# Linear attention by pairs of token tiles, with the output gates applied where the output projection's operand is made

## The chip, the cores and the metric

The kernel runs on one core of a Trainium2 chip. The metric is the time of one execution in device microseconds; the time before is the median of three runs. The engines are named as in the profile: PE (matmul; PEld its weight loads), DVE (elementwise, vector), ACT (activation functions and copies), POOL, and SP, which here issues most DMAs.

## The reference

One encoder layer for 1024 prompt tokens and 64 sample tokens (1088 in all, width 1024). A modulated RMS norm, one input projection, two mixers side by side, one output projection, and a squared-ReLU MLP of 4096. What matters here is the second mixer, gated linear attention with 4 heads, keys of 64 and values of 128, and what follows it:

```
b = cumsum(log_a); scores = q k exp(b_t - b_s), causal
o = scores v + (q exp(b)) state
state = state exp(b_end) + (k exp(b_end - b))^T v
o = rms_norm(o) * silu(r)
x = x + gate1 * (concat[attention, o] @ w_out)
```

Everything is float32; large products are made of three products of rounded halves.

## The kernel before

Activations lie with features on the partitions. Tokens are worked in tiles of 128 (`TILES`, eight of the prompt and one of 64 for the sample). Large matmuls go through `mm3` (L91 to L95): each operand is split into a rounded high part (ACT copy, L101) and a rest (DVE difference, L102), and three matmuls add up.

The order of the work is made by `interleave` (L46). Each stream of work is a generator that yields an estimate of PE time, a wait, and a condition; the first stream in the list that may go on goes on. The stage in question (L842) has the streams weights, `gla` (linear attention), `main` (projection of values and gate inputs, groups B0 and B1), `gate_cols` (projection of r, groups C0 and C1, stored to the DRAM tensor `r_d`), `gates`, and `latents` (group D1, which may run on into the next stage). The framework then orders the instructions of each queue from this priority and their dependences; the engines and SP work their queues in order. `load_group` (L195) brings a weight group through three raw buffers and splits it into one of two operand buffers.

`gla` works one tile at a time. `main` gives it the cumulated log gates `bcum`. For each of seven levels (halves of 64, 32, ... 1 tokens) `prep` forms the difference of b to a reference (L686), its exponentials for keys (L691) and, by head halves, for queries (L694), and multiplies them with keys (L696) and queries (L703). The query operand `QL` holds zeros in the other head's half of the partitions, so that one matmul serves two heads. Two matmuls (L755) give scores, of which a masked copy (L763; for the first level an ACT copy, L760) puts the blocks that belong to this level into `ST`. After the levels come the output (L798, L802), its norm (L807 to L810), and in `tail` a transposition and a store to the DRAM tensor `mix_d` (L816 to L820). The recurrent state is updated at the third level (L775 to L784).

`gates` (L828) waits for all of that in the planner, and then, tile by tile, loads r and the mix from DRAM, makes silu (L837) and product (L838), and stores the mix again (L839). The two loads use the buffers of the values (`gv`).

The next stage makes the keys of the past (`past_keys`: transposition L1074, split L1080 and L1081, products in `keys_values`) and the query latents (`query_main`). Then follows attention. Near its end `out_early` (L1190) loads the first quarter of the mix (272 tokens) in three pieces into the raw buffers, splits them, and begins four column blocks of the output projection while attention ends. The other three quarters are loaded (L1326, L1327), split (L1344, L1345) and multiplied in `main` of the output projection (L1319).

## Time and profile before

| what | us |
|---|---|
| median of three runs (1381.74 to 1384.07) | 1383.76 |
| the profiled execution's own time | 1381.47 |
| its span | 1379.7 |
| PE busy in the span | 1333.5 |
| DVE busy | 903.7 |
| ACT busy | 700.6 |
| PE busy from 95 to 285 (190 us, linear attention) | 186.35 |
| PE busy from 285 to 330 (45 us, its end and the next stage's begin) | 27.53 |
| PE busy from 440 to 600 (160 us, attention) | 157.00 |
| PE busy from 600 to 700 (100 us, output projection) | 100.00 |

A busy PE is a matmul in flight; the stretch that stands out is the one from 285 to 330. In the profile's rows a group shows its line, engine, operation, output and inputs with their shapes, the count, the busy time and the mean of one, and then the idle time of the engine before them with what ended it.

### The profile page before, as it was taken

To read this page: it belongs to the slowest core of one execution; us is meant where nothing else is said; L and a number is where in the kernel's file an instruction comes from. 1 tells how busy PE (TensorE), PEld (TensorE's weight loads), DVE (VectorE), ACT (ScalarE), POOL (GpSimd) and SP (SyncE) were. 2 spreads that over 40 slices of the span, in tenths; PEclk is the share of its full clock that TensorE was granted. 3 is DMA by queue.
4 is the path that set the end of the run, shared out by engine and by line. 5 is a ranking of instruction groups with operands and counts; after the bars stand their busy time and mean duration, and the time that the engine had idled before them with its cause. 6 is when DMAs were issued, how large, how long until landed. Compare 5 with 4: busy or idle time off the path is not lost.

```text
span 1379.7 us, 26169 instructions
## 1 busy us (share of the span) xinstructions
PE 1333.5 (97%) x10020; PEld 1256.7 (91%) x10020; DVE 903.7 (65%) x2041; ACT 700.6 (51%) x1768; POOL 61.9 (4%) x115
## 2 busy tenths in 40 slices
PE   7999999959999999999999999999999999999998
PEld 5898899948866779899999999999999999999998
DVE  5787876746475756756799756656645866864554
ACT  5466766963255656744474444444434343434332
POOL 0010000111011110000000000000000000000000
PEclk9999999989999999999999999999999999999999
DMA  9420315552154431364406444444249855543440
GB/s 344 127 74 1 89 55 151 151 153 81 58 176 125 160 113 41 85 187 128 139 23 204 161 133 160 136 142 154 97 160 322 277 197 168 174 124 99 123 130 33
DMA packets 166167, 188.14 MB, mean 136 GB/s; under 512 B 16878, under 2 KB 117530, under 8 KB 166042
## 3 DMA queue, kind: packets, MB, share of 16 engines
q1 hardware_dynamic: 158586, 180.90, 41.6%
q10 hardware_dynamic: 7456, 5.57, 1.3%
q8 instruction: 79, 1.29, 0.4%
q14 instruction: 46, 0.38, 0.1%
HBM read 132.97 MB, written 53.46 MB: 135 GB/s over the span
## 4 chain that ended last, share of the span: by engine, by line
PE 83%; DVE 6%; ACT 4%; DMA 3%; issue 2%; POOL 1%; SPq 0%; ACTq 0%; DVEq 0%; POOLq 0%
PE mm L93 15%; PE mm L95 14%; PE mm L94 14%; PE g L93 6%; PE g L95 6%; PE g L94 5%; PE tp L93 3%; PE tp L95 3%; PE tp L94 3%; PE mm L1000 3%; PE g L1027 2%; PE mm L166 2%; PE g L755 1%; PE tp L1037 1%; DVE al L102 1%
## 5 line engine op out<-in xcount | busy, mean ns | idle before, releaser
L101 ACT CAST opers<-quad 128x512 fp32r<-128x512 f32 x112 | 69.5, 621 | 184.6 <-PE mm L95 145.0
L102 DVE TENSOR_TENSOR opers<-quad,opers 128x512 fp32r<-128x512 f32 x112 | 77.2, 690 | 113.7 <-ACT opers L101 113.7
L93 PE MATMUL mm<-opers 128*128 128x272 f32 x448 | 128.7, 287 | 0.3 <-DVE e L1816 0.3
L95 PE MATMUL mm<-opers 128*128 128x272 f32 x448 | 128.9, 288 | 0.0
L94 PE MATMUL mm<-opers 128*128 128x272 f32 x448 | 128.3, 286 | 0.0
L93 PE MATMUL mm<-ah,wh 128*128 128x272 f32 x424 | 122.4, 290 | 2.7 <-ACT wh L101 1.3
L94 PE MATMUL mm<-al,wh 128*128 128x272 f32 x424 | 121.6, 288 | 0.3 <-DVE al L102 0.3
L95 PE MATMUL mm<-ah,wl 128*128 128x272 f32 x424 | 121.5, 288 | 0.0
L93 PE MATMUL mm<-hh,wh 128*128 128x384 f32 (+2 forms) x264 | 91.8, 350 | 0.3 <-ACT hh L101 0.3
L94 PE MATMUL mm<-hl,wh 128*128 128x384 f32 (+2 forms) x264 | 88.0, 333 | 0.0
L95 PE MATMUL mm<-hh,wl 128*128 128x384 f32 (+2 forms) x264 | 87.4, 331 | 0.0
L93 PEld LDWEIGHTS mm<-opers 128*128 128x128 f32 x448 | 84.6, 189 | 0.5 <-issue 0.5
L95 PEld LDWEIGHTS mm<-opers 128*128 128x128 f32 x448 | 84.3, 188 | 0.0
L94 PEld LDWEIGHTS mm<-opers 128*128 128x128 f32 x448 | 84.1, 188 | 0.0
L93 PEld LDWEIGHTS mm<-ah,wh 128*128 128x128 f32 x424 | 79.8, 188 | 4.0 <-ACT wh L101 1.9
L94 PEld LDWEIGHTS mm<-al,wh 128*128 128x128 f32 x424 | 79.7, 188 | 0.5 <-DVE al L102 0.5
L95 PEld LDWEIGHTS mm<-ah,wl 128*128 128x128 f32 x424 | 79.5, 188 | 0.2 <-DVE wl L102 0.2
L102 DVE TENSOR_TENSOR opers<-ru,opers 128x544 fp32r<-128x544 f32 x108 | 77.6, 719 | 2.2 <-ACT opers L101 2.0
L101 ACT CAST opers<-ru 128x544 fp32r<-128x544 f32 x108 | 69.5, 644 | 13.1 <-PE mm L95 11.7
L101 ACT CAST wh<-ru 128x512 fp32r<-128x512 f32 x67 | 41.2, 618 | 65.3 <-PE g L94 24.5
L102 DVE TENSOR_TENSOR wl<-ru,wh 128x512 fp32r<-128x512 f32 x67 | 45.9, 689 | 35.6 <-ACT wh L101 35.4
L93 PE MATMUL mm<-wh,hh 128*128 128x264 f32 (+3 forms) x216 | 66.8, 311 | 0.0
(410 smaller groups left out, 4316.7 us busy)
## 6 DMA issues: line engine op xcount, KB each, us to landing
ru<-u_d SPq DMA_DIRECT2D x108, 272.0 KB, 2.9
raw<-in_w_ada SPq DMA_DIRECT2D x40, 512.0 KB, 3.9
ru<-in_w_up SPq DMA_DIRECT2D x32, 512.0 KB, 4.2
quad<-in_w_down SPq DMA_DIRECT2D x16, 1024.0 KB, 7.6
u_d<-st SPq DMA_DIRECT2D x60, 272.0 KB, 2.1
u_d<-sc SPq DMA_DIRECT2D x45, 272.0 KB, 2.1
raw<-in_w_in SPq DMA_DIRECT2D x22, 256.0 KB, 4.6
x<-in_xo_T SPq DMA_DIRECT2D x8, 544.0 KB, 5.4
```

The lines of the kernel that those rows point to most:

```text
L93: PE.matmul(out, lhsT=ah, rhs=bh, start=first, stop=False, skip_group_check=more)
L94: PE.matmul(out, lhsT=ah, rhs=bl, start=False, stop=False, skip_group_check=more)
L95: PE.matmul(out, lhsT=al, rhs=bh, start=False, stop=last, skip_group_check=more)
L101: ACT.copy(hi, src)
L102: eng.tensor_tensor(out=lo, in0=src, in1=f32(hi), op=ALU.subtract)
L166: mm = PE.matmul(acc[32 * j:32 * j + 32, 0:256], lhsT=scT[:, k, :], rhs=was[k][:, 256 * j:256 * (j + 1)], start=(k == 0), stop=(k == KT - ...
L755: PE.matmul(sc[:n, p, :, :n // 2], lhsT=kl[:, n * p:n * p + n], rhs=ql[:, :, p, :n // 2], start=True, stop=True)
L1000: PE.matmul(sp[:n, :w], lhsT=x[:, hd, :n], rhs=y[:, hd, :w], start=(j == 0), stop=(j == 4))
L1027: PE.matmul(op[:n, 0:P], lhsT=pt[:kw, k, :n], rhs=kvs[kt // 4].v[:kw, kt % 4, hd], start=(kt == 0), stop=(kt == nkt - 1))
L1037: PE.transpose(tp[:kw, k, :n], pr[k0 // 4][:n, P * k:P * k + kw], ident[:n, :n])
```

## The change

The linear attention takes two tiles in one turn (`UNITS`; the sample's tile alone). `prep` makes one difference over both tiles and two exponentials in place; `factors` multiplies the key part in place and writes the query part, head half by head half, into zero-padded `QL` buffers of full length; four matmuls fill a whole bank with scores of both tiles, and one masked copy takes them. The state is updated between the tiles of a pair. `main` projects B1 (gates and half of the values) before B0, and marks values and gates apart. q and k are laid out by pairs, so that an eviction of 384 columns is written in pieces. `load_group` issues its raw loads before it waits for operand buffers. The stream `gates` is gone: `out_early` and the output projection's `main` load r beside the mix and apply silu and product before they split the operand; in `out_early` the operand comes in six pieces instead of three. The core of the diff:

```diff
+UNITS = [(0, 1), (2, 3), (4, 5), (6, 7), (8,)]
...
-    def load_group(key, src, nk, n, step=2, after=None, pool=None):
-
-        if after is not None:
-            yield 300, 0, after
-        wh = (pool or wp).tile([P, nk, n], F32R, name="wh")
-        wl = (pool or wp).tile([P, nk, n], F32R, name="wl")
+    def load_group(key, src, nk, n, step=2, after=None, pool=None, early=None):
+
         units = [(k, min(step, nk - k)) for k in range(0, nk, step)]
         raws = {}
 
...
             raws[u] = rawp.tile([P, kn, n], F32, name="raw")
             SP.dma_start(raws[u], src[k * P:(k + kn) * P].rearrange("(k p) n -> p k n", p=P))
 
+        if early is not None:
+            yield 300, 0, early
         for u in range(min(3, len(units))):
             load(u)
         yield 0, 4000, None
+        if after is not None:
+            yield 0, 0, after
+        wh = (pool or wp).tile([P, nk, n], F32R, name="wh")
+        wl = (pool or wp).tile([P, nk, n], F32R, name="wl")
...
-    GROUPS = [("A0", 704, 960), ("A1", 960, 1216), ("B0", 1216, 1480), ("B1", 1480, 1744), ("C0", 1744, 2000),
+    GROUPS = [("A0", 704, 960), ("A1", 960, 1216), ("B1", 1480, 1744), ("B0", 1216, 1480), ("C0", 1744, 2000),
               ("C1", 2000, 2256), ("D1", 384, 704)]
 
     def loader():
         for j, (key, a, b) in enumerate(GROUPS):
             if j >= 2:
-                yield from load_group(key, w_in_cols(a, b), 8, b - a, after=has("end " + GROUPS[j - 2][0]))
+                yield from load_group(key, w_in_cols(a, b), 8, b - a, after=has("end " + GROUPS[j - 2][0]),
+                                      early=has("shift") if j == 2 else None)
         yield from load_group("UK", I["w_ukv"], 2, 1024, step=1, after=has("end C1"))
-        yield from load_group("UQ", I["w_uq"], 3, 768, step=1, after=has("end D1"))
+        yield from load_group("UQ", I["w_uq"], 3, 768, step=1, early=has("end D1"))
...
-                        ACT.activation(qk_place((i + 2) % 4, c0, c0 + cn), by_tile(ps, c0), AF.Copy,
-                                       scale=0.125 if g == 0 else 1.0)
+                        for a, b in pieces(c0, c0 + cn):
+                            ACT.activation(qk_place((i + 2) % 4, a, b), ps[:, a - c0:b - c0], AF.Copy,
+                                           scale=0.125 if g == 0 else 1.0)
...
-        KL = [big.tile([P, 2 * P], F32, name=f"KL{j}") for j in range(3)]
-        QL = [big.tile([P, 2, 2, 64], F32, name=f"QL{j}") for j in range(3)]
         SBk = [big.tile([P, 2, 256], F32, name=f"SB{i}") for i in range(3)]
-        for t in KL + QL + SBk:
+        QL = [big.tile([P, 2, 2 * P], F32, name=f"QL{j}") for j in range(2)]
+        for t in QL + SBk:
...
         def main():
-            yield 0, 0, has("B0")
+            turn = 0
+            yield 0, 0, has("B1")
             for c in range(3):
                 c0, cn = CHUNKS[c]
                 tl = [(i, off, n) for i, (off, n) in enumerate(TILES) if c0 <= off < c0 + cn]
-                for i, off, n in tl:
-                    ps = yield from rows("B0", off, n, 264)
-                    gvs[i] = gw.tile([P, 512], F32, name="gv", bufs=9)
-                    ACT.copy(gvs[i][:n, 0:264], ps)
-                yield 1500, 0, has("B1")
-                glr = glrT[c % 2]
-                for part in (tl[:1], tl[1:]) if c == 0 else (tl,):
+                for part in (tl[:2], tl[2:]) if c < 2 else (tl,):
+                    glr = glrT[turn % 2]
+                    turn += 1
+                    t0, tn = part[0][1], sum(n for _, _, n in part)
                     for i, off, n in part:
                         ps = yield from rows("B1", off, n, 264)
-                        DVE.tensor_copy(gvs[i][:n, 264:512], ps[:, 0:248])
-                        gl = sm.tile([P, 16], F32, name="gl")
+                        gvs[i] = gw.tile([P, 512], F32, name="gv", bufs=7)
+                        gl = spare[:, 16 * (i % 4):16 * (i % 4) + 16]
                         DVE.tensor_copy(gl[:n], ps[:, 248:264])
+                        ACT.copy(gvs[i][:n, 264:512], ps[:, 0:248])
                         tp = tp_bank()
                         PE.transpose(tp[0:16, 0:n], gl[:n], ident[:n, :n])
-                        DVE.tensor_copy(glr[0:16, off - c0:off - c0 + n], tp[0:16, 0:n])
-                    t0, tn = part[0][1], sum(n for _, _, n in part)
+                        DVE.tensor_copy(glr[0:16, off - t0:off - t0 + n], tp[0:16, 0:n])
                     for p in range(2):
                         z = g_bank()
-                        PE.matmul(z[:, :tn], lhsT=wg[:, p * P:(p + 1) * P], rhs=glr[:, t0 - c0:t0 - c0 + tn],
+                        PE.matmul(z[:, :tn], lhsT=wg[:, p * P:(p + 1) * P], rhs=glr[:, 0:tn],
                                   start=True, stop=True)
                         a = gw.tile([P, 384], F32, name="sq")
                         ACT.activation(a[:, :tn], z[:, :tn], AF.Abs)
...
                             DVE.tensor_tensor_scan(bcum[:, p, off:off + n], ones[:, :n], a[:, off - t0:off - t0 + n],
                                                    0.0, op0=ALU.mult, op1=ALU.add)
                     done.update(f"gates {i}" for i, _, _ in part)
+                for i, off, n in tl:
+                    yield 0, 0, has("B0")
+                    ps = yield from rows("B0", off, n, 264)
+                    ACT.copy(gvs[i][:n, 0:264], ps)
+                    done.add(f"v {i}")
...
                 def prep(hf):
 
 
+                    bv = b.rearrange("p c (x y) -> p c x y", y=2 * hf)
+                    ref = bv[:, :, :, hf - 1:hf].broadcast_to([P, 2, w // (2 * hf), 2 * hf])
+                    d = gw.tile([P, 4 * P], F32, name="dd", bufs=3)[:, 0:2 * w]
+                    DVE.tensor_tensor(out=d.rearrange("p (c x y) -> p c x y", c=2, y=2 * hf), in0=bv, in1=ref, op=ALU.subtract)
+                    dv = d.rearrange("p (x r h) -> p x r h", r=2, h=hf)
+                    for r in range(2):
+                        ACT.activation(dv[:, :, r], dv[:, :, r], AF.Exp, scale=(2 * r - 1) / 16.0)
+                    return d, hf
+
+                def factors(d, hf):
+
                     nonlocal rot
-                    bv = b.rearrange("p c (x y) -> p c x y", y=2 * hf)
-                    ref = bv[:, :, :, hf - 1:hf].broadcast_to([P, 2, n // (2 * hf), 2 * hf])
-                    dd = gw.tile([P, 2 * P], F32, name="dd", bufs=3)[:, 0:2 * n]
-                    DVE.tensor_tensor(out=dd.rearrange("p (c x y) -> p c x y", c=2, y=2 * hf), in0=bv, in1=ref, op=ALU.subtract)
-                    ds, dt = roles(dd, hf)
-                    kl, ql = KL[rot % 3][:, 0:2 * n], QL[rot % 3]
+                    ql = QL[rot % 2]
                     rot += 1
-                    ks, _ = roles(kl, hf)
-                    ACT.activation(ks, ds, AF.Exp, scale=-1.0 / 16)
+                    dv = d.rearrange("p (x r h) -> p x r h", r=2, h=hf)
+                    kv, qv = (kq[:, 2 * w * r:2 * w * r + 2 * w].rearrange("p (x r h) -> p x r h", r=2, h=hf)[:, :, r]
+                              for r in range(2))
+                    DVE.tensor_tensor(out=dv[:, :, 0], in0=dv[:, :, 0], in1=kv, op=ALU.mult)
                     for j in range(2):
-                        ps = slice(64 * j, 64 * j + 64)
-                        ACT.activation(ql[ps, j, :, :n // 2].rearrange("p c (b h) -> p c b h", h=hf),
-                                       dt[ps].rearrange("p (c b) h -> p c b h", c=2), AF.Exp, scale=1.0 / 16)
-                    DVE.tensor_tensor(out=ks, in0=roles(kq[:, 0:2 * n], hf)[0], in1=ks, op=ALU.mult)
-                    qt = roles(kq[:, 2 * n:4 * n], hf)[1]
-                    for c in ((0, 2),) if n == P else ((0, 1), (1, 2)):
-                        c0, c1 = c
-                        qv = ql[:, :, c0:c1, :n // 2].rearrange("p j c (b h) -> p j (c b) h", h=hf)
-                        nb = n // (2 * hf)
-                        q1 = qt[:, c0 * nb:c1 * nb].rearrange("p (o x) h -> p o x h", o=1).broadcast_to([P, 2, (c1 - c0) * nb, hf])
-                        DVE.tensor_tensor(out=qv, in0=qv, in1=q1, op=ALU.mult)
-                    return kl, ql
-
-                pr = gw.tile([P, 2, P], F32, name="pr", bufs=1)
-                DVE.tensor_tensor(out=pr[:, :, :n], in0=q, in1=k, op=ALU.mult)
+                        rs = slice(64 * j, 64 * j + 64)
+                        DVE.tensor_tensor(out=ql[rs, j, 0:w].rearrange("p (x h) -> p x h", h=hf), in0=dv[rs, :, 1],
+                                          in1=qv[rs], op=ALU.mult)
+                    return d, ql
...
+                kts = []
+                yield 300, 1000, None
+                for lv, hf in enumerate(halves):
+                    (d, ql), nb = ready.pop(0), n // (2 * hf)
+                    if lv + 2 < len(halves):
+                        ready.append(prep(halves[lv + 2]))
+                    if lv + 1 < len(halves):
+                        ready[0] = factors(*ready[0])
+                    if lv + 2 == len(halves):
+                        if u + 1 < len(UNITS) and can(u + 1)():
+                            begun = begin(u + 1)
+                    elif lv + 1 == len(halves) and begun is not None:
+                        begun[6][0] = begun[3](*begun[6][0])
+                        begun[6].append(begun[2](begun[5][1]))
+                    sc = g_bank()[:, 0:2 * w].rearrange("p (a c j t) -> p a c j t", a=nt, c=2, j=2)
+                    qv = ql[:, :, 0:w].rearrange("p j (c a t) -> p j c a t", c=2, a=nt)
+                    for a in range(nt):
+                        for p in range(2):
+                            PE.matmul(sc[:n, a, p], lhsT=d[:, w * p + n * a:w * p + n * a + n], rhs=qv[:, :, p, a],
+                                      start=True, stop=True)
+                    src = sc[:n].rearrange("p a c j (b h) -> p (a c j) b h", h=hf)
+                    to = ST[:n, 0:nt, :, :n].rearrange("p a g t -> p (a g) t").rearrange("p g (b r h) -> p r g b h", r=2, h=hf)[:, 1]
+                    if nb == 1:
+                        ACT.copy(to[:hf], src[:hf])
+                    else:
+                        mlv = 5 - (hf.bit_length() - 1)
+                        DVE.copy_predicated(to, masks[:n, mlv, :n // 2].rearrange("p (o b h) -> p o b h", o=1, h=hf)
+                                            .broadcast_to([n, 4 * nt, nb, hf]), src)
+                    yield 900, 2200, None
+                    if lv < nt:
+                        tp = tp_bank()
+                        for p in range(2):
+                            PE.transpose(tp[:n, P * p:P * p + P], kk[:, p, n * lv:n * lv + n], ident)
+                        kts.append(gw.tile([P, 256], F32, name="kt_", bufs=2))
+                        ACT.copy(kts[lv][:n], tp[:n, 0:256])
+                    if lv == 2:
+                        i = tl[0]
+                        yield 0, 0, has(f"v {i}")
+                        olds = (SBk[2], SBk[1]) if i == 8 else (SBk[i % 2], SBk[(i + 1) % 2])
+                        state(i, n, 0, E1, kts[0], *olds)
+                    if lv >= 3 and tails:
+                        tail()
...
-        def gates():
-
-            yield 0, 2000, has("end C1", "gla out")
-            for i, (off, n) in enumerate(TILES):
-                r, mx = (gw.tile([P, 512], F32, name="gv", bufs=9) for _ in range(2))
-                SP.dma_start(heads(r)[:, :, :n], r_d[:, :, off:off + n])
-                SP.dma_start(heads(mx)[:, :, :n], mix_d[:, 4:8, off:off + n])
-                yield 0, 1000, None
-                r, mx = (heads(t)[:, :, :n] for t in (r, mx))
-                ACT.activation(r, r, AF.Silu)
-                (DVE if i % 2 else DVE).tensor_tensor(out=r, in0=r, in1=mx, op=ALU.mult)
-                SP.dma_start(mix_d[:, 4:8, off:off + n], r)
-
         lats = Stream(latents())
-        interleave([weights, gla(), main(), gate_cols(), gates(), lats], rest=(weights, lats))
+        interleave([weights, gla(), main(), gate_cols(), lats], rest=(weights, lats))
...
+    def gate(t, r):
+        ACT.activation(r, r, AF.Silu)
+        DVE.tensor_tensor(out=t, in0=t, in1=r, op=ALU.mult)
+
     def out_early():
         yield 1000, 0, has("wo 4")
         mixh.append(wctx.enter_context(tc.tile_pool(reuse_waits="tile", name="mixh", bufs=1, side="right")))
         mh, ml = mix_pair()
         mixh.append((mh, ml))
-        ks = ((0, 3), (3, 3), (6, 2))
-        raws = []
-        for k, kn in ks:
+        def fetch(src, k, kn):
             t = rawp.tile([P, kn, HW], F32, name="raw")
-            SP.dma_start(t, mix_d[:, k:k + kn, 0:HW])
-            raws.append(t)
+            SP.dma_start(t, src[:, k:k + kn, 0:HW])
+            return t
+
+        def halves(k, kn, t):
+            split(mh[:, k:k + kn], ml[:, k:k + kn], t, DVE)
+
+        t0, t1, r1 = fetch(mix_d, 0, 3), fetch(mix_d, 4, 2), fetch(r_d, 0, 2)
         yield 0, 3000, None
-        for (k, kn), t in zip(ks, raws):
-            split(mh[:, k:k + kn], ml[:, k:k + kn], t, DVE)
+        halves(0, 3, t0)
+        gate(t1, r1)
+        halves(4, 2, t1)
+        t2, r2, t3 = fetch(mix_d, 6, 2), fetch(r_d, 2, 2), fetch(mix_d, 3, 1)
+        yield 0, 3000, None
+        gate(t2, r2)
+        halves(6, 2, t2)
+        halves(3, 1, t3)
...
+                mx.append(xw.tile([P, 4, HW], F32, name="mr", bufs=1))
                 for _, t0, n, o in parts:
+                    SP.dma_start(mx[2][:, :, o:o + n], r_d[:, :, t0:t0 + n])
...
+                    gate(mx[1], mx[2])
```

225 lines of the change are left out of this document (110 added, 115 removed).

## The prediction

> **What bounds the kernel now.** I read the page first, then the busy time of each engine by stretches, then PE's waits where PE is not full, then the order of time there.
>
> ```profile
> span 1379.7 us, 26169 instructions
> PE 1333.5 (97%) x10020; PEld 1256.7 (91%) x10020; DVE 903.7 (65%) x2041; ACT 700.6 (51%) x1768; POOL 61.9 (4%) x115
> ```
>
> PE is busy 97% of the span, so this change, which takes no matmul away, can win only where PE stands still or runs slowly. The table of stretches (length, busy time of PE, PEld, DVE, ACT, POOL, then PE's clock) says where that is:
>
> ```profile
> 95.00:285.00 190.00, 186.35 (x1302) 175.44 (x1302) 141.00 (x410) 138.97 (x466) 16.89 (x34) 1.00 0.31 89
> 285.00:300.00 15.00, 9.18 (x59) 6.73 (x59) 8.65 (x20) 11.90 (x36) 2.64 (x6) 0.90 0.58 157
> 300.00:310.00 10.00, 1.22 (x2) 0.50 (x2) 2.61 (x5) 3.16 (x10) 0.00 (x0) 0.50 0.73 192
> 310.00:330.00 20.00, 17.13 (x88) 14.74 (x89) 13.65 (x37) 6.54 (x28) 2.67 (x4) 0.90 0.31 88
> 330.00:350.00 20.00, 19.75 (x118) 17.80 (x117) 12.96 (x32) 8.03 (x30) 2.66 (x4) 1.00 0.31 93
> 350.00:440.00 90.00, 86.69 (x566) 65.60 (x565) 50.83 (x155) 37.60 (x142) 9.30 (x14) 0.98 0.37 114
> ```
>
> The linear-attention stage (95 to 285) leaves PE idle for 3.65 us in 190: other streams' projections fill it. Right behind it PE is idle 5.82 + 8.78 + 2.87 + 0.25 = **17.7 us** between 285 and 350, the only large hole after the start-up. What it waits for, and the order of time in it:
>
> ```profile
> PE g L95 <- DVE latl L1081: 7.7, 1, 7.7
> PE tp L816 <- DVE og L810: 5.0, 1, 5.0
> ```
>
> ```profile
> 297.24 0.68 DVE L810 TENSOR_TENSOR og<-mm,s 64x512 f32<-64x512 f32 x1 [2.88 <-POOL s L121]
> ...
> 300.77 0.46 SPq L820 DMA_DIRECT2D mix_d<-mog  x1
> ...
> 304.58 0.36 SPq L834 DMA_DIRECT2D gv<-mix_d  x1
> ...
> 307.66 0.42 DVE L838 TENSOR_TENSOR gv<-gv 128x256 f32<-128x256 f32 x1 [2.37 <-DMA gv<-mix_d]
> ...
> 308.12 1.14 ACT L213 CAST wh<-raw 128x512 fp32r<-128x512 f32 x2 [1.37 <-DVE gv L838]
> ...
> 310.18 0.42 DVE L1081 TENSOR_TENSOR latl<-tp,lath 128x256 fp32r<-128x256 f32 x1 [1.83 <-DMA mix_d<-gv]
> ```
>
> This is a chain through the sample tile: the last linear-attention output (L810), its store to DRAM (L820), its reload by the gates stage (L834), the gate's product (L838), and only then the next stage's weight split (L213, which takes over the gates' buffers) and key split (L1081). Before it PE ran out of filler while the linear attention was still going: its outputs come at an even, slow pace, and the last is at 297.2.
>
> ```profile
> L810 DVE TENSOR_TENSOR og<-mm,s x9: 683/692/694, 124.1 to 297.2; 128x512 f32<-128x512 f32 x8, 64x512 f32<-64x512 f32 x1
> ```
>
> Eight intervals from 124.1 to 297.2 are 21.6 us per tile. So two things make the hole: the linear attention ends last, and the gates stage hangs behind its end.
>
> **The change part by part.** *The pair loop.* These rows carry it (columns: instructions, busy us, mean ns):
>
> ```profile
> L694 ACT ACTIVATE QL<-dd 64x128 f32<-64x128 f32 x112 | 34.1, 304 | 1.2
> ...
> L763 DVE COPY_PREDICATED ST<-masks,g 128x256 f32<-128x256 int32 x48 | 25.7, 536 | 5.0 <-PE g L755 4.6
> L703 DVE TENSOR_TENSOR QL<-QL,gqk 128x256 f32<-128x256 f32 x56 | 23.6, 422 | 5.4 <-ACT QL L694 4.5
> L686 DVE TENSOR_TENSOR dd<-bcum 128x256 f32<-128x256 f32 x56 | 22.6, 417 | 0.0
> ...
> L691 ACT ACTIVATE KL<-dd 128x128 f32<-128x128 f32 x56 | 17.5, 313 | 14.1 <-PE g L755 13.3 <-DVE dd L686 0.4
> ...
> L696 DVE TENSOR_TENSOR KL<-gqk,KL 128x128 f32<-128x128 f32 x56 | 16.3, 291 | 1.8 <-ACT KL L691 1.2
> ...
> L837 ACT ACT_TABLE_LOAD x7 | 9.0, 1283 | 0.1
> ...
> L838 DVE TENSOR_TENSOR gv<-gv 128x512 f32<-128x512 f32 x8 | 5.5, 687 | 2.4 <-ACT gv L837 2.2 <-DMA gv<-mix_d 0.2
> L691 ACT ACT_TABLE_LOAD x6 | 7.7, 1283 | 0.5 <-DVE ST L763 0.4
> ...
> L713 ACT ACTIVATE E<-bcum 128x256 f32<-128x256 f32 x8 | 3.3, 418 | 2.1 <-DVE bcum L613 1.1 <-DVE SB L784 0.8
> ...
> L837 ACT ACTIVATE gv<-gv 128x512 f32<-128x512 f32 x8 | 5.1, 633 | 0.6 <-DMA gv<-r_d 0.6
> ```
>
> A level of one tile costs DVE 0.417 + 0.291 + 0.422 + 6/7 of 0.536 = 1.59 us (one level of seven goes to ACT instead), so two tiles 3.18, and ACT 2 x (0.313 + 2 x 0.304) = 1.84. A level of a pair is one 128x512 difference (0.687, row L838), one 128x256 key product and two 64x256 query products (0.422 each, row L703; the trace has no product of 256 elements on 64 partitions), 6/7 of a masked copy, and on ACT two 128x256 exponentials (0.418 each, row L713). No masked copy of 512 elements is in the trace: it costs at least 0.536 + (0.687 - 0.417) = 0.81 if only the longer stream counts, at most 2 x 0.536 = 1.07; I take 0.94. That is DVE 0.687 + 3 x 0.422 + 0.81 = 2.76 us (2.65 to 2.87), ACT 0.84. Over 28 pair levels DVE saves 28 x 0.42 = 12 us and ACT 28 us; ACT also loses 13 table loads, 13 x 1.283 = 16.7 us, and nine gates of about 0.63. PE issues the same matmuls with the same columns (four of 128 per pair level instead of two of 128 per tile level), so PE's 186 us in this stage stay. What shrinks is the linear attention's length. The stage's DVE work falls from 141 us by these 12 and by nine gate products of 0.687 to about 123. If DVE were the bound and never waited, nine tiles would come at 13.7 us each; now they come at 21.6. I take 17, between the ends since the chain still passes through four engines: 34 us a pair. Tile 0's loop began one interval before its output, at about 102; four pairs and the sample's 22 end at 102 + 136 + 22 = 260, and with one pair waiting a little for its gates at 270, before PE's filler ends at about 285. Within the stage I count nothing gained or lost: its 3.65 us of gaps could vanish or, with the denser loop, double (bounds: 3.6 gained, 3.6 lost).
>
> *The gates stage goes.* Its nine reloads of the mix, nine of r and nine stores leave SP, and the chain from 300.77 to 310.18 has nothing to hang on. What is late next at the boundary is the key split itself, behind its own transposes, with the latent projections as PE's cover, since they are last in the streams' order and now fall across the boundary. The remaining idle time is between 0 and 17.7 us; the nearest other stretch that holds a boundary, 350 to 440, has 90 - 86.69 = 3.3 us in it. I take 2.5.
>
> *The slow clock goes with the hole.* After the idle time PE's matmuls came at half pace:
>
> ```profile
> 312.53 0.63 PE L93 MATMUL g<-wh,lath 128*128 128x512 f32 x1
> 312.96 0.63 PE L94 MATMUL g<-wl,lath 128*128 128x512 f32 x1
> ...
> 314.12 0.39 PE L94 MATMUL g<-wl,lath 128*128 128x512 f32 x1
> 314.35 0.39 PE L95 MATMUL g<-wh,latl 128*128 128x512 f32 x1
> ```
>
> Starts are 0.43 us apart at 312.5 and 0.23 at 314.1. The clock column's 0.90 over the 20 us from 310 means 4 us at half speed; some 3 of them are matmuls, which at full pace take half: 1.5 us saved, if no long idle time is left.
>
> *Weights, gates' columns first, evictions by pieces.* The raw loads start before their operand buffers are free, which can only bring them earlier; an eviction of 384 columns becomes two, about 0.2 us of ACT more for eight of them, under PE's full stretch. Nothing.
>
> *The gate where the output operand is made.* In the three later chunks it adds a load of r, one silu of 1088 elements (1.1 us, as the cast at 617.08 below) and one product (1.29, as the ml<-mx row below). That second chunk's operand is split from about 601 on and PE gets to it at 617.08, where the first chunk's last matmul ends; so about 10 us of matmuls cover the 2.4 us, which would be lost in each chunk without them. The first chunk is tighter:
>
> ```profile
> L93 PE MATMUL mm<-mh,wh x152: 283/289/394, 588.3 to 685.2; 128*128 128x272 f32 x152
> ...
> L102 DVE TENSOR_TENSOR ml<-mx,mh x6: 1281/1285/1294, 602.4 to 645.8; 128x1088 fp32r<-128x1088 f32 x6
> ...
> L102 DVE TENSOR_TENSOR ml<-raw,mh x3: 707/1001/1009, 582.0 to 587.0; 128x816 fp32r<-128x816 f32 x2, 128x544 fp32r<-128x544 f32 x1
> ```
>
> ```profile
> 617.08 1.10 ACT L101 CAST mh<-mx 128x1088 fp32r<-128x1088 f32 x1 [2.00 <-PE mm L95]
> ```
>
> ```profile
> DMA to landing us min/median/max: 3.3/4.5/5.0
> ```
>
> Now all three pieces are split by 587.7 and PE begins at 588.3. With six pieces through three buffers, the second three loads wait for buffers to come free: a landing of 4.5 us, a silu of about 0.65, a product, a cast and a difference of about 0.7 each, and a table load of 1.28, some 8 us: ready at about 596. Head block 3 comes last, and PE needs it fourth. SP's queue behind those loads holds the last w_out columns and the next chunk's operands, which then come some 7 us later into slack of about 10. The four chunks' 4 x 192 matmuls run from 588.3 to past 685.2, 0.126 us each, so the first chunk's 24.2 us leave about 4.5 of the 28.8 to 617.08 for the last attention products. These, and blocks 0 to 2 of up to four banks (36 matmuls, 4.5 us), PE can do while it waits, if they are ordered so: a stall of 0 to 7 us. I take 2, near the covered end.
>
> Here a rule of the Trainium skill speaks against the change. In the trace a table load shows 1.283 us and nothing around it:
>
> ```profile
> 230.74 0.46 ACT L625 COPY cq<-mm 128x384 f32<-128x384 f32 x1
> 231.21 1.28 ACT L691 ACT_TABLE_LOAD   x1
> 232.51 0.31 ACT L691 ACTIVATE KL<-dd 128x128 f32<-128x128 f32 x1
> ```
>
> The copy ends at 231.20, the load follows at once and the next exponential starts at 232.51. The Trainium skill, "ScalarE: Activation LUTs", section "What ACT_TABLE_LOAD costs", counts a further drain of about 1.38 us, 2.66 us for each change of set. Two changes there and back between the last softmax exponentials and the first silus are 4 x 1.28 = 5.1 us by the rows and 10.6 by the page, which would put 5 us more into this corner; the row decides, so I leave the sum as it is.
>
> **Sum.** -17.7 - 1.5 + 2.5 + 2 = **-14.7 us**: a span of 1365.0, and 1366.8 with the 1.8 that the profiled run has around its span (1381.47 against 1379.7). The median of the runs is 2.3 above the profiled run, so on its scale 1383.76 - 14.7 = **1369 us**.
>
> **The rivals.** *(A) The linear attention still ends last* (or the boundary keeps most of its hole): for it, the loop is a chain of DVE, ACT, PE and DVE, and at twice the width each link is longer; against it, of 21.6 us a tile some 6 are not DVE work (141 busy / 9 is 15.7), and such waits come once for two tiles now. Then only the part behind 297 goes, about 10 of the 17.7, and 2 come back: about 1376. *(B) Slower: PE stands in its queue behind the pair's factors.* A level's four matmuls now wait for a product that comes after a wider difference and wider exponentials, and PE takes nothing past them. At 34 levels, 0.45 us each eats the 14.7; at 0.6 us it is 34 x 0.6 - 14.7 = +6, 1390. Against it: now the 62 tile levels cost PE no more than 3.65 us together, and ACT loses a third of its work. *(C) The hole belongs to the next stage:* its own loads and key chain end at the same time without the gates, so only the clock and a few us move and the first-chunk stall takes them: 1383. The row at 308.12, released by the gate's product, speaks against it. *(D) More:* no hole, no stall, the 3.65 us gone as well: 1383.76 - 17.7 - 1.5 - 3.6 = 1361.
>
> **How the numbers follow.** Forecast 0.52 (1363 to 1374), A 0.20, D 0.09, C 0.08, B 0.11. A measurement of this kernel tells about 0.2%, 2.8 us, from no change. Faster: forecast, A, D and a quarter of C, 0.83; same 0.06; slower 0.11. The range takes in D's edge and A's and most of C: 1360 to 1382.
>
> **What would show it.** Right: the last og product (L810's successor) starts before 270 instead of 297; PE busy over 95% in every stretch between 285 and 330 of the old time, clock 1.00; no table loads in the linear-attention stage and a handful near the output projection; its operands' first matmuls within 4 us of idle time. Wrong: PE waits on the new query products of more than 10 us in total (B), a hole as large behind an earlier end (C), or og still the last event of its stage (A).

## The result, and the profile after

The changed kernel takes 1369.52 us (median of four runs, 1368.94 to 1371.51) beside 1382.75 for the kernel before on the same chip: 0.9919 of it, 95% interval 0.9901 to 0.9938. Run again in a later set it took 1368.00, 0.9908 (0.9893 to 0.9922); 0.9905 to 0.9935 had been expected of that set, with a wait of PE on the sum of squares, shown below, of 2 to 3 us, where it was 1.7. The forecast was 1369. The profiled execution of the changed kernel is the slowest of its four (1371.51); where it matters, the second set's profile stands beside it.

The head of the page of the changed kernel:

```profile
span 1369.6 us, 25859 instructions
PE 1333.4 (97%) x10024; PEld 1258.9 (92%) x10024; DVE 894.2 (65%) x1931; ACT 661.0 (48%) x1651; POOL 64.8 (5%) x111
```

PE's busy time is what it was (1333.5); ACT has 40 us less to do. The gain is where PE stood. The same stretches as shown of the kernel before (length, then busy PE, PEld, DVE, ACT, POOL, then PE's clock, DMA share, GB/s):

```profile
95.00:285.00 190.00, 184.44 (x1297) 172.79 (x1296) 139.12 (x328) 102.31 (x368) 16.34 (x28) 1.00 0.24 69
285.00:300.00 15.00, 12.26 (x77) 10.66 (x77) 8.70 (x21) 5.76 (x26) 4.99 (x8) 1.00 0.18 49
300.00:310.00 10.00, 10.00 (x64) 9.28 (x63) 5.73 (x16) 4.76 (x19) 2.08 (x4) 1.00 0.21 57
310.00:330.00 20.00, 18.93 (x118) 16.54 (x117) 12.57 (x28) 9.86 (x33) 3.63 (x6) 1.00 0.28 79
330.00:350.00 20.00, 20.00 (x133) 19.97 (x131) 5.12 (x16) 3.04 (x6) 0.00 (x0) 1.00 0.38 133
350.00:440.00 90.00, 87.28 (x567) 62.09 (x570) 51.93 (x155) 39.72 (x151) 11.82 (x16) 0.96 0.44 135
```

Between 285 and 350 PE is idle 2.74 + 0 + 1.07 + 0 = 3.8 us instead of 17.7, and its clock stays at 1.00. The row of the linear attention's outputs (least, median and longest duration in ns, first and last start) says why:

```profile
L774 DVE TENSOR_TENSOR og<-mm,s x9: 683/692/693, 131.7 to 262.5; 128x512 f32<-128x512 f32 x8, 64x512 f32<-64x512 f32 x1
```

Its last output starts at 262.5 instead of 297.2, while PE still has the latent projections to do. The groups of the pair loop, with mean durations in ns behind the bar:

```profile
L713 DVE TENSOR_TENSOR QL<-dd,gqk 64x256 f32<-64x256 f32 x56 | 23.3, 417 | 0.4
L845 DVE COPY_PREDICATED ST<-masks,g 128x512 f32<-128x512 int32 x24 | 22.0, 918 | 3.2 <-PE g L837 2.9
L699 ACT ACTIVATE dd<-dd 128x256 f32<-128x256 f32 x56 | 21.3, 422 | 20.3 <-DVE dd L696 15.4 <-DVE spare L606 3.6 <-PE g L738 1.1
L696 DVE TENSOR_TENSOR dd<-bcum 128x512 f32<-128x512 f32 x28 | 19.3, 688 | 1.2 <-PE g L837 1.0
...
L710 DVE TENSOR_TENSOR dd<-dd,gqk 128x256 f32<-128x256 f32 x28 | 11.8, 421 | 2.6 <-ACT dd L699 2.3
```

A level of a pair costs DVE 0.688 + 0.421 + 2 x 0.417 + 6/7 x 0.918 = 2.73 us.

How far the gain lives on can be read from four milestones: the first matmul of the query projection, the first of the output projection, the last of attention (a product of values and probabilities), and the last with the late w_out columns (`woh`).

| | before | changed | changed, second set |
|---|---|---|---|
| first query product | 383.6 | 366.2 (-17.4) | 364.9 (-18.7) |
| first output-projection matmul | 588.3 | 573.1 (-15.2) | 569.8 (-18.5) |
| last matmul of attention | 594.8 | 581.5 (-13.3) | 578.2 (-16.6) |
| last matmul with `woh` | 694.3 | 684.1 (-10.2) | 680.2 (-14.1) |
| span | 1379.7 | 1369.6 (-10.1) | 1365.5 (-14.2) |

Up to the first output matmul attention keeps the gain or loses 2 us of it; that differs from run to run. The output projection gives back 4.4 to 5.0 us in both: from its first matmul to its last with `woh` it takes 111.0 and 110.4 us, before 106.0. Attention and output projection overlap, so this split depends on the mark: the first output matmul now comes 8.4 us ahead of attention's last, before 6.5. By attention's last matmul 4.1 and 2.1 us are given back up to it, and 3.1 and 2.5 behind it. The sum from the first query product on, 7.2 and 4.6 us, is the same by both marks. PE's waits in the changed kernel from 565 to 625 (total, times, longest):

```profile
PE tp L1432 <- DVE acc L1418: 2.2, 1, 2.2
PE tp L1069 <- ACT prob L1043: 0.9, 1, 0.9
```

L1432 sums up the squares of the first output chunk for the second norm. In order of time, PE and then ACT of the changed kernel around that wait (start, duration, and in brackets the idle time before and what ended it):

```profile
605.76 0.29 PE L96 MATMUL mm<-mh,wl 128*128 128x272 f32 x1
608.23 0.71 PE L1432 MATMUL tp<-ones,acc 128*128 128x1 f32 x6 [2.19 <-DVE acc L1418]
...
609.73 0.29 PE L94 MATMUL mm<-mh,wh 128*128 128x272 f32 x1
...
610.47 0.43 PE L95 MATMUL mm<-ml,wh 128*128 128x272 f32 x1
610.70 0.43 PE L96 MATMUL mm<-mh,wl 128*128 128x272 f32 x1
```

```profile
606.18 1.11 ACT L1223 ACTIVATE mr<-mr 128x1088 f32<-128x1088 f32 x1 [2.20 <-DMA mr<-r_d]
607.20 0.41 ACT L1417 ACTIVATE sq<-x 128x272 f32<-128x272 f32 x1
607.52 1.08 ACT L102 CAST mh<-mx 128x1088 fp32r<-128x1088 f32 x1
```

The square at 607.20 is the last of the first chunk, and its input had been there since 604.9. It stands in ACT's queue behind a silu, and that silu belongs to the third chunk and waits for its load of r. The column sums are in PE's queue, the adding up of the squares in DVE's, square and silu in ACT's, each worked in order, so PE stands although the second chunk's operand has been ready since 603.1. Behind the wait matmuls start 0.23 us apart instead of 0.126: 16 steps take 3.5 us instead of 2.0, some 1.5 us more.

### The profile page after: what moved, and what is told of

It is laid out like the page before. It is cut to its first block, busy times and chain, and to the rows that moved or that the text cites. A ratio compares the mean times of both kernels' runs of the same rounds, so it can differ in the third digit from the quotient of the medians.

```text
span 1369.6 us, 25859 instructions
## 1 busy us (share of the span) xinstructions
PE 1333.4 (97%) x10024; PEld 1258.9 (92%) x10024; DVE 894.2 (65%) x1931; ACT 661.0 (48%) x1651; POOL 64.8 (5%) x111
## 4 chain that ended last, share of the span: by engine, by line
PE 82%; DVE 7%; DMA 4%; ACT 4%; issue 1%; POOL 1%; SPq 0%; ACTq 0%; DVEq 0%; POOLq 0%
PE mm L94 14%; PE mm L96 14%; PE mm L95 14%; PE g L94 6%; PE g L96 5%; PE g L95 5%; PE tp L94 3%; PE tp L95 3%; PE tp L96 3%; PE mm L1032 3%; PE g L1059 2%; PE g L837 2%; PE mm L167 2%; PE tp L1069 1%; DMA mr<-r_d 1%
```

## The experiments

All twelve in one table, each against the kernel before on its own chip. "Idle" is PE's from 285 to 350, "output" the time from the first output matmul to the last with `woh`, "wait" PE's on the sum of squares; the times are us. A kernel that ran once has no interval. The kernel without the silu table and the two with the gate on one side only leave out part of the gate.

| kernel | median | ratio (95%) | idle | output | wait |
|---|---|---|---|---|---|
| before | | 1 | 17.7 | 106.0 | 0 |
| changed | 1369.52 | 0.9919 (0.9901 to 0.9938) | 3.8 | 111.0 | 2.2 |
| changed, second set | 1368.00 | 0.9908 (0.9893 to 0.9922) | 3.8 | 110.4 | 1.7 |
| pairs, gates stage kept | 1369.43 | 0.9927 (0.9911 to 0.9942) | 6.2 | 106.1 | 0 |
| single tiles, gates at the output | 1378.83 | 0.9989 (0.9980 to 0.9999) | 9.2 | 110.5 | 1.8 |
| changed, one tile in a turn | 1386.00 | 1.0038 (1.0020 to 1.0055) | 11.3 | 111.0 | 2.2 |
| changed, late raw loads | 1368.30 | 0.9906 (0.9885 to 0.9928) | 2.8 | 110.7 | 1.9 |
| no silu table in the first quarter | 1370.43 | 0.9927 (0.9913 to 0.9941) | 3.6 | 109.1 | 3.4 |
| silu in program order | 1371.68 | 0.9934 (0.9921 to 0.9947) | 3.8 | 113.1 | 2.8 |
| gate in the first quarter only | 1366.58 | one run | 3.8 | 107.2 | 0 |
| gate in the later chunks only | 1364.62 | one run | 3.8 | 106.2 | 0.5 |
| second chunk's loads from POOL | 1374.51 | 0.9952 (0.9938 to 0.9967) | 3.8 | 115.6 | 5.4 |
| third chunk behind the squares | 1366.28 | 0.9899 (0.9880 to 0.9918) | 3.8 | 107.3 | 0 |
| and silu at r's eviction | 1367.42 | 0.9901 (0.9885 to 0.9918) | 3.8 | 103.7 | 0 |

### Which half of the change closes the hole?

Two kernels take the change apart. The first keeps everything but the move of the gates:

```diff
-        interleave([weights, gla(), main(), gate_cols(), lats], rest=(weights, lats))
+        interleave([weights, gla(), main(), gate_cols(), gates(), lats], rest=(weights, lats))
...
-                    gate(mx[1], mx[2])
```

> The changed kernel, with the old gates stage put back (nine reloads, silus, products and stores behind each tile's linear attention) and the output projection's operand made as before. Theory 1, the hole stood because linear attention ended last: the pair loop still ends near 262, the nine gates run under the latent projections that PE still has until about 285 to 290, so the hole stays closed, and the 5 us that the output projection lost come back: 1364 to 1370, not slower than the changed kernel. Theory 2, the hole stood because of the gates stage's store and reload in front of the next stage's splits: of 17.7 us some 9 stay, the output part wins 5: 1373 to 1379, with PE idle 8 us or more between 265 and 330. Table loads: about 10 in the stage again.

The second is the kernel before with the gates alone moved:

```diff
-        interleave([weights, gla(), main(), gate_cols(), gates(), lats], rest=(weights, lats))
+        interleave([weights, gla(), main(), gate_cols(), lats], rest=(weights, lats))
...
+                    gate(mx[1], mx[2])
```

> The kernel before, with only the gates moved: no gates stage, r loaded and silu and product made where the output projection's operand is made; linear attention tile by tile as before. Theory 1: the last linear-attention output stays near 290 to 297, PE still stands 8 us or more between 285 and 310; only the part behind 300.8 (8 to 9 us) goes, and the output part pays 5: 1376 to 1381. Theory 2: the hole closes as in the changed kernel: 1367 to 1372.

Stretches of the kernel of pairs with the gates stage:

```profile
285.00:300.00 15.00, 12.98 (x75) 11.19 (x75) 11.92 (x34) 6.38 (x25) 1.34 (x2) 1.00 0.67 192
300.00:310.00 10.00, 8.20 (x49) 6.73 (x48) 6.63 (x15) 5.88 (x20) 3.65 (x6) 1.00 0.29 91
310.00:330.00 20.00, 17.90 (x108) 15.83 (x108) 14.54 (x35) 9.65 (x39) 3.84 (x6) 1.00 0.41 118
```

Outputs and stretches of the kernel of single tiles with the gates at the output:

```profile
L810 DVE TENSOR_TENSOR og<-mm,s x9: 682/692/693, 122.3 to 295.4; 128x512 f32<-128x512 f32 x8, 64x512 f32<-64x512 f32 x1
```

```profile
285.00:300.00 15.00, 9.01 (x50) 6.29 (x49) 8.49 (x18) 8.97 (x33) 1.94 (x4) 0.74 0.56 145
300.00:310.00 10.00, 8.13 (x45) 6.92 (x43) 6.80 (x19) 4.07 (x15) 1.35 (x2) 0.88 0.66 189
```

With pairs alone the hole shrinks from 17.7 to 6.2 us, the clock stays up, and the time is the changed kernel's within the intervals (0.9927 against 0.9919 and 0.9908): the pair loop, with the companions that this kernel keeps, is the gain, and what the move of the gates adds to it is not measurable. With the gates alone moved the hole loses 8.5 us, the part behind 300, as theory 1 had it; but linear attention still ends at 295.4, PE stands 6 us before 300, and the output projection pays 4.5 us for what it took over: 0.9989 is at the edge of no change. The two halves multiply to 0.9927 x 0.9989 = 0.9916, which is the changed kernel's ratio within its interval. Of the table loads expected in the first kernel's stage there is only one: with the gates behind the end of linear attention, ACT no longer swaps between silu and exponentials.

### Is it the pair's width, or what came with it?

```diff
-UNITS = [(0, 1), (2, 3), (4, 5), (6, 7), (8,)]
+UNITS = [(i,) for i in range(9)]
...
```

> The changed kernel with one tile in a turn instead of two (q and k laid out by tiles), all else as changed: gates at the output, in-place factors, B1 first, early raw loads. Theory, the pair's width is what makes linear attention end early: the pace goes back to 20 to 22 us a tile, the last output to about 285 to 297, PE stands 8 us or more between 285 and 330, and the time is 1375 to 1381. Rival, the in-place form, the order of B1 and B0 and the early loads do most of it: the last output before 270 and 1367 to 1371.

Outputs of this kernel, and the largest waits of DVE and ACT in it from 110 to 285:

```profile
L774 DVE TENSOR_TENSOR og<-mm,s x9: 683/692/692, 125.5 to 306.2; 128x512 f32<-128x512 f32 x8, 64x512 f32<-64x512 f32 x1
```

```profile
DVE ST L845 <- PE g L837: 13.1, 17, 1.6
```

```profile
ACT dd L699 <- DVE dd L696: 27.2, 33, 2.6
```

The new form at the old width is slower than the kernel before: 22.6 us a tile, the last output at 306.2, 1386 us, outside the expected 1375 to 1381 on the slow side. Between 95 and 285 DVE is no busier than in the other two (139.2 us, 141.0 before, 139.1 with pairs) and has got less far; it waits for PE's scores 17 times, and ACT for DVE's differences 33 times (with pairs 6 and 15 times, from 110 to 262). Part of the loss is DVE's own work: a level of a single tile costs it 0.420 + 0.289 + 2 x 0.283 + 6/7 x 0.537 = 1.74 us in this form, two of them 3.47 against a pair's 2.73, which is 2.6 us a tile over seven levels, of the 6.2 between 22.6 and 16.4 us a tile. In the form of the kernel before a level was 1.59, so at the old width the new form is the worse one. The other 3.6 us are not DVE's work. These waits read as a chain from DVE to ACT, PE and back to DVE, which each tile passes singly at every level and a pair once for two tiles; no run tests that reading by itself, and none undoes the order of B1 and B0 alone.

The other companion, raw loads before the operand buffers are free, undone:

```diff
+        if after is not None:
+            yield 300, 0, after
+        wh = (pool or wp).tile([P, nk, n], F32R, name="wh")
+        wl = (pool or wp).tile([P, nk, n], F32R, name="wl")
         units = [(k, min(step, nk - k)) for k in range(0, nk, step)]
...
-        if early is not None:
-            yield 300, 0, early
```

> The changed kernel with the weight groups' raw loads issued as in the kernel before (after the wait for the operand buffers, and for the query weights after the end of the latents' group). Theory, these loads were put at nothing: within 1.5 us of the changed kernel's 1368.0. Rival, the early loads are what keeps PE supplied between 285 and 330 and at the start of linear attention: 3 to 8 us more, with PE idle at the starts of the groups.

0.9906, as the changed kernel: the early loads are worth nothing that can be measured, as the prediction put them.

### What does the output projection pay for?

First the table loads. They stand among attention's last exponentials (ACT of the changed kernel):

```profile
568.51 1.28 ACT L1223 ACT_TABLE_LOAD   x1 [0.55 <-DMA raw<-r_d]
569.81 0.66 ACT L1223 ACTIVATE raw<-raw 128x544 f32<-128x544 f32 x1
570.48 1.28 ACT L1043 ACT_TABLE_LOAD   x1
```

```diff
-        gate(t1, r1)
+        gate(t1, r1, AF.Exp)
...
-        gate(t2, r2)
+        gate(t2, r2, AF.Exp)
```

> The changed kernel with exp in place of silu in the first quarter of the output operand (its result is then not the gate): no table of silu is loaded before attention's last softmax. Theory, by the rows: two table loads of 1.28 us go from between the softmax exponentials, and with them the 0.9 us for which PE waited for a probability at 570 to 575: 1 to 2 us less than the changed kernel, 1367.5 to 1368.5. Rival, a drain of 1.38 us stands around each load: 4 to 5 us less. Other rival: the wait at 570 is the end of attention and not the table: no change.

The wait of 0.9 us on a probability is gone and no other has come near 570, so the tables made it. But the time, 1370.43, is not the expected 1367.5 to 1368.5: PE now waits 3.4 us at L1432. DVE and ACT of this kernel there:

```profile
601.87 1.29 DVE L1224 TENSOR_TENSOR mx<-mx,mr 128x1088 f32<-128x1088 f32 x1 [2.73 <-DMA x_d<-x]
603.08 0.50 DVE L1410 SCALAR_TENSOR_TENSOR x<-mm,modT,x 128x272 f32<-128x272 f32 x1
```

```profile
603.67 0.43 ACT L1417 ACTIVATE sq<-x 128x272 f32<-128x272 f32 x1 [2.91 <-DVE x L1410]
```

Here nothing stands ahead of the last square in ACT's queue; its input is late, because DVE's queue has the third chunk's gate product (L1224), which waits for a DMA, ahead of the eviction (L1410) that makes this input.

Then that wait itself. The first attempt held only the silu back:

```diff
-                    gate(mx[1], mx[2])
+                    tc.keep_in_program_order(ACT.activation(mx[2], mx[2], AF.Silu))
+                    DVE.tensor_tensor(out=mx[1], in0=mx[1], in1=mx[2], op=ALU.mult)
```

> The changed kernel, with the silu of the three later output chunks held in program order on ACT, so that it cannot come ahead of the square of the last block of an earlier chunk while it waits for its load of r. Theory: PE's 2.2 us of idle time at 605.8 (its column sums waiting for a square that stands behind that silu) and the half clock behind it (1.7 us at 610 to 615) go: 3 to 4 us less than the changed kernel, 1365 to 1367. Rival: the next chunk's operand is late in any case, or the wait moves to the product or the cast: within 1 us of the changed kernel.

The rival held in kind: PE still waits, 2.8 us now, and the time is 1371.68, above the changed kernel's by more than the 1 us that the rival allowed. ACT of this kernel, at the same place:

```profile
606.10 1.10 ACT L102 CAST mh<-mx 128x1088 fp32r<-128x1088 f32 x1 [2.27 <-DMA mx<-mix_d]
607.10 0.42 ACT L1418 ACTIVATE sq<-x 128x272 f32<-128x272 f32 x1
```

The silu is behind the square now, but the next in line, the cast of the third chunk, stands ahead of it and waits for its own load. So not the silu as such, but work of the third chunk that stands ahead of the square on ACT, or of its input on DVE, does it, as long as its loads come late. Why are they late? SP's queue in the kernel before and then in the changed one:

```profile
583.07 5.01 SPq L1159 DMA_DIRECT2D raw<-in_w_out  x3
588.17 1.53 SPq L1333 DMA_DIRECT2D x<-in_xo_T  x2
589.80 1.38 SPq L1326 DMA_DIRECT2D mx<-mix_d  x1
```

```profile
578.98 3.13 SPq L1191 DMA_DIRECT2D raw<-in_w_out  x3
582.22 2.07 SPq L1380 DMA_DIRECT2D x<-in_xo_T  x2
584.38 0.66 SPq L1372 DMA_DIRECT2D mr<-r_d  x1
...
600.61 1.20 SPq L1372 DMA_DIRECT2D mr<-r_d  x2
```

Against the first output matmul (588.3 and 573.1) the second chunk's first load is issued 1.5 us behind it before, and 11.3 us behind it after: 9.8 us later (7.9 against attention's last matmul), since the first quarter goes twice through the three raw buffers and w_out's loads wait for these, with everything behind them. The third chunk's r then waits for the one buffer `mr`, which is free when the second chunk's product is made (600.6). Two kernels leave the gate out on one side. The gate in the first quarter only:

```diff
-                    SP.dma_start(mx[2][:, :, o:o + n], r_d[:, :, t0:t0 + n])
...
-                    gate(mx[1], mx[2])
```

> The changed kernel, whose three later output chunks are left without the gate (no r load, silu or product there); the first quarter keeps it in six pieces. Theory, the first quarter's second round through the three raw buffers makes all that follows on SP late: PE still waits 1.5 us or more near 605. Rival, the later chunks' own r loads and silus make the wait: no wait near 605, while the 1 us near 570 stays.

The gate in the later chunks only, and the first quarter in three pieces:

```diff
+        ks = ((0, 3), (3, 3), (6, 2))
...
-        t0, t1, r1 = fetch(mix_d, 0, 3), fetch(mix_d, 4, 2), fetch(r_d, 0, 2)
...
-        gate(t1, r1)
-        halves(4, 2, t1)
...
```

> The changed kernel, whose first output quarter is left without the gate and goes through in three pieces as in the kernel before; the three later chunks keep it. Theory: no wait of PE over 0.5 us between 565 and 625, and a span 3 to 5 us shorter than the changed kernel's. Rival, the later chunks' own r loads and silus make it: PE still waits 1.5 us or more near 605.

The wait is 0 us without the later gates and 0.5 without the first quarter's. Each run by itself points to the half that it left out, so neither half makes the wait alone: it needs the delay of SP's queue by the one and the later chunks' own r loads by the other, and each without the other is inside the slack. The theory that the first quarter does it alone falls with the first of the two.

Next the queue was to be passed by:

```diff
-                    load(WORDER[w + 1])
+                    load(WORDER[w + 1], POOL if w == 0 else SP)
```

> The changed kernel, with the loads of the second output chunk (r and both halves of the mix) issued from POOL's queue instead of SP's, where they stand behind three w_out loads that wait for the raw buffers of the first quarter. Theory, SP's queue is what makes the second and third chunk late: these loads start near 577 instead of 584, the third chunk's follow earlier too, and PE's wait on the sum of squares near 605 (2.2 us) and the half clock behind it (1.8 us) go: 3 to 4 us less than the changed kernel. Rival, the DMA engines are full there (share 1.06 to 1.12 from 585 to 595): the loads only trade places with those of w_out and x, and the wait stays at 2 us or turns up at the x rows or w_out's cast: within 1 us.

It is 6.5 us slower than the changed kernel, which neither theory had. POOL's queue in it:

```profile
579.12 0.96 POOL L1372 DMA_DIRECT2D mr<-r_d  x1 [34.35 <-DMA raw<-in_w_out]
587.20 0.79 POOL L1373 DMA_DIRECT2D mx<-mix_d  x1 [7.13 <-issue]
591.73 0.76 POOL L1374 DMA_DIRECT2D mx<-mix_d  x1 [3.73 <-issue]
```

The first load, released by a DMA of w_out, goes out at 579.1, 1.5 us ahead of the same load in the changed kernel's second profile (580.6), so SP's queue is hardly passed by. The three loads go out 8.1 and 4.5 us apart, where SP issues them within 2 us; why POOL takes so long, the profile does not show. The second chunk's operand is complete 30.2 us after the first output matmul, in the changed kernel 30.0 and 29.7: no earlier. But the order of ACT's queue had changed with it, and both the silu and the first cast of the third chunk now stand ahead of the last square, which runs at 606.27; DVE's queue has the third chunk's product ahead of the last adding up, which runs at 607.47. PE waits 5.4 us.

That left the order of the queue itself. A data dependence puts the third chunk behind the squares, with no change to what is computed (`first` is the first chunk's sum of squares):

```diff
+                    if w == 2:
+                        late = nw.tile([P, 1], F32, name="late", bufs=1)
+                        DVE.tensor_scalar(out=late, in0=first[:, 0:1], scalar1=0.0, scalar2=None, op0=ALU.mult)
+                        ACT.activation(mh[:, 0:4], mx[0], AF.Identity, bias=late)
...
+                        ACT.activation(mx[2], mx[2], AF.Silu, bias=late)
```

> The changed kernel, with the first cast and the silu of the third output chunk made to wait for the first chunk's sum of squares (a bias of zero worked out from that sum), so that neither can stand ahead of the last square in ACT's queue; its first half is cast by an Identity activation. Theory, the wait near 605 is ACT's queue order alone: the last square runs at once, PE's wait on the sum (1.7 to 2.2 us in the changed kernel) and the half clock behind it (1.7 us) go, and the third chunk, cast some 3 us later, is still ready 20 us before PE needs it: 3 to 4 us less than the changed kernel's 1368.0, 1364 to 1365, faster than both kernels. Rival, the second chunk's own operand is late and PE would wait there next: PE idle near 605 to 610 as before, within 1 us of 1368.

ACT of this kernel:

```profile
601.35 0.43 ACT L1427 ACTIVATE sq<-x 128x272 f32<-128x272 f32 x1 [1.83 <-DVE x L1420]
602.76 0.43 ACT L1427 ACTIVATE sq<-x 128x272 f32<-128x272 f32 x1 [0.98 <-DVE x L1420]
604.39 1.21 ACT L1394 ACTIVATE mh<-mx,late 128x1088 fp32r<-128x1088 f32 x1 [1.20 <-DMA mx<-mix_d]
```

The last square runs at once, the load is waited for behind it, and PE's wait and the half clock are gone; from the first output matmul to the last with `woh` it is 107.3 us, 3.1 less than in the changed kernel's second profile; from attention's last matmul on it is 98.9 us, against 102.6 and 102.0 in the changed kernel and 99.5 before. This shows the mechanism. In the time, which had been expected at 1364 to 1365, 1366.28 (0.9899) against 1368.00 and 1369.52 (0.9908 and 0.9919) is 1.7 to 3.2 us, and the intervals overlap: it is the lowest median of all with the gates computed, and no measured improvement over the changed kernel.

Last, silu where r is evicted, for the tokens that the first quarter needs, on top of the previous kernel:

```diff
-                        (ACT.copy if c0 else DVE.tensor_copy)(r[:, :cn], ps)
+                        if c0:
+                            ACT.copy(r[:, :cn], ps)
+                        else:
+                            ACT.activation(r[:, :cn], ps, AF.Silu)
```

> The kernel of the previous run (third output chunk behind the squares), with the silu of r for the first 384 tokens made where r is evicted from PSUM (four evictions of 384 columns, as silu instead of a copy), so that the first output quarter needs only the product and the third chunk silu only for the rest of its tokens. No table of silu is loaded while attention's softmax still runs. Theory: four of the table loads move to the linear-attention stage, doubled to eight of 1.28 us, where ACT is busy 102 of 190 us and linear attention ends 20 us before PE's other work does, and cost nothing there; PE's wait of 0.9 to 1.5 us on a probability near 570 goes, and with it some 1 us: 1364.5 to 1366, 0.988 to 0.990 of the kernel before, the best of all. Rival, the eight loads hold up linear attention's exponentials: the last output after 270, PE idle near 265 to 300, and 1367 to 1372.

Linear attention bears the eight table loads (last output 264.2, idle 3.8 us as before), so that rival is out; but the time is 1367.42, no better and outside the expected 1364.5 to 1366. ACT of this kernel where the tables had been:

```profile
570.24 0.65 ACT L102 CAST mh<-raw 128x544 fp32r<-128x544 f32 x1 [1.33 <-DVE raw L1245]
570.98 0.78 ACT L1046 ACTIVATE prob<-mm,sta,ssq 128x512 f32<-128x512 f32 x1
```

The cast of the gated piece now waits at the head of ACT's queue for DVE's product, and the exponential behind it with it: PE still waits 0.7 us for the probability. (Its short "output" in the table comes from a first output matmul that PE takes 6 us later; from attention's last matmul on it is 100.5 us.)

## Why the prediction was right, point by point

**The bound.** PE-bound, won only where PE stands or runs slowly: PE's busy time over the span is the same to 0.1 us in both pages, and the whole gain is idle time.

**The pair loop.** A level was put at 2.76 us of DVE, it is 2.73; the masked copy of 512, bounded at 0.81 to 1.07 and taken as 0.94, measures 0.918. The pace was taken as 17 us a tile, 34 a pair: the first outputs of the four pairs start at 131.7, 171.8, 202.5 and 234.7, on average 34.3 us apart, and by all nine outputs the pace is (262.5 - 131.7) / 8 = 16.4. The end was taken as 260, it is 262.5. So rival A (linear attention still ends last) did not happen. That the loop gains by its width beyond the work that it saves, on which both A and the forecast rested, is what the one-tile kernel shows. Rival B (PE behind the pair's factors): PE's waits on the score operands (L837) come to 1.1 us in the whole stage, against a mark of 10, and none of it is for a query product. In the one-tile form, though, they are 7.1 us: the mechanism exists, at the other width.

**The hole.** Predicted -17.7 + 2.5, measured 17.7 to 3.8, so 1.3 less. One sign that the prediction named was missed with it: PE over 95% busy in every stretch; from 285 to 300 it is 12.26 of 15 us, 82%. The two causes that the prediction read from the chain are both real: without the chain behind 300.8 the hole loses 8.5 us, with the shorter loop 11.5, with both 13.9. Both runs together come to more than 13.9, so part of the hole goes by either. Rival C (the next stage's own hole) falls.

**The slow clock.** This term was mis-sized: -1.5. From the start to the first query product, in the kernel before and then the changed one:

```profile
0.00:383.60 383.60, 351.20 (x2407) 318.23 (x2407) 259.44 (x701) 228.19 (x697) 33.94 (x74) 0.98 0.39 118
```

```profile
0.00:366.20 366.20, 345.96 (x2410) 316.55 (x2410) 244.16 (x585) 181.07 (x572) 35.34 (x70) 1.00 0.34 105
```

The same matmuls keep PE busy 5.2 us less, at a clock of 1.00 against 0.98, and PE is idle 12.2 us less: together the 17.4. How much of the 5.2 is the clock alone, these rows don't split; by the end of the span as much busy time has come back, some 1.5 of it in the half clock described above. The stage's own gaps, put at nothing within 3.6, cost 1.9 (5.56 us idle against 3.65; in the second set 4.78). To the first query product the prediction's terms are -16.7 and the runs -17.4 and -18.7.

**The output projection.** Put at +2 and expected in the first chunk; it is +4.4 to +5.0 by the first output matmul, +2.5 to +3.1 by attention's last, and of another make. The first chunk did stall for only 0.9 to 1.1 us, through table loads between the exponentials, and matmuls of other banks covered the late operand as foreseen. The sentence that failed is that SP's queue makes the next chunk's operands "come some 7 us later into slack of about 10": they come 7.9 to 9.8 us later, by the mark that is taken, and the operands do fit in the slack, but in ACT's queue, in front of a square that PE needs, stands work of the chunk after the next, whose loads are later still. That is the 1.7 to 2.2 us of wait and some 1.5 of half clock behind it; some 1.3 us are left of the 5.0 and 4.4, and they are also there in the kernel with the third chunk behind the squares (107.3 against 106.0), and by attention's last matmul nothing is left there. The prediction followed the late loads to the operand that needs them and not to what stands behind that operand's first instruction in its engine's queue.

**The table loads.** By the rows, 1.28 us each with nothing around them, against 2.66 in the Trainium skill, "ScalarE: Activation LUTs", section "What ACT_TABLE_LOAD costs". The silu at 569.81 starts 0.02 us after its load ends and the next load at 570.48, 0.01 us after that silu: the trace agrees with the rows and shows no drain. Three loads came at this corner, not four.

**The sum.** -17.4 or -18.7 to the first query product, 7.2 or 4.6 back behind it, where 2 had been put: -10 to -14 between the profiles, -13.2 and -13.6 between the medians, and the forecast -14.7. The errors, a larger clock term and a larger return, went against each other; that the time was hit better than its terms were is luck.

## What to carry to other kernels

A loop that passes from engine to engine at every step can gain by width more than the work that the width saves; test the width alone before crediting the rest. Work moved to a place where it is hidden still takes a place in an in-order queue: look for the first instruction there that waits for a load, and at what stands behind it, also for a chunk that nobody needs yet. And a stall that is taken away moves on until the last queue that can hold it is in order; the profile shows that sooner than the time does.

## What the runs showed of the hardware

- Between 555 and 640 us PE fell to half pace after waits of 1.7 us (second set: clock 0.66 from 605 to 610), 1.8, 1.9, 2.0, 2.2, 2.8, 3.4 and 5.4, and kept its full pace through waits of 0.9, 1.2, 1.4 and 1.5. That is no general limit: in the changed kernel a wait of 1.07 us, ended at 411.32 among shorter matmuls, is followed by a clock of 0.50 from 412 to 418. In the changed kernel the slow matmuls behind the wait of 2.2 us begin 1.6 us after PE has started again (608.23 to 609.85) and last 3.5 us. The Trainium skill, "TensorE: Matmul & The Clock Gate", section "What's actually happening", puts the half rate behind at least one idle window of about 3.4 us; the 3.5 us of slow matmuls are about as long as that window, but waits of half of it, and at 411 of a third of it, sufficed here.
- In the one run with such loads, three of 544 KB issued by POOL went out 8.1 and 4.5 us apart, by SP 0.7 and 1.1 us apart; an issue on POOL took 0.8 to 1.0 us and 3.7 to 7.1 us of idle time lay before the second and the third.
- A masked copy of 128x512 takes 0.918 us, of 128x256 0.536: 1.7 times for twice the elements, where the plain difference goes from 0.417 to 0.688, 1.65 times.
